# The hybrid mixer in one written order: convolution taps spread over the attention, split scores

## The chip, the cores and the metric

The kernel runs on one core of a Trainium2 chip. The metric is the device time of one execution in microseconds (us), from the first instruction to the last. Its engines each take their own instructions strictly in their own order: PE (TensorE, matrix products; its weight loads are listed as PEld), DVE (VectorE), ACT (ScalarE), POOL (GpSimd) and SP (which here only issues transfers). They wait for each other by semaphores. An instruction that waits holds back everything that stands behind it on its engine.

## The reference

The program is a two layer decoder trunk over 512 tokens of width 1024, all in float32. The change touches one part only, the mixer of layer 0, which is attention beside a convolution module:

```python
def hybrid_mixer(h, cos, sin, w_in, dw_w, dw_b, ln_g, ln_b, w_out):
    proj = h @ w_in
    q = apply_partial_rotary(heads(proj[..., :A_WIDTH]), cos, sin)
    k = apply_partial_rotary(heads(proj[..., A_WIDTH:2 * A_WIDTH]), cos, sin)
    v = heads(proj[..., 2 * A_WIDTH:3 * A_WIDTH])
    for window, dilation in DILATED_PATTERNS:
        o_g, lse_g = dilated_window_branch(q, k, v, window, dilation)
...
    u = proj[..., 3 * A_WIDTH:]
    glu = u[..., :CONV_CHANNELS] * jax.nn.sigmoid(u[..., CONV_CHANNELS:])
    c = causal_depthwise_conv(glu, dw_w) + dw_b
    c = jax.nn.silu(layer_norm(c, ln_g, ln_b))
    return jnp.concatenate([attn, c], axis=-1) @ w_out
```

There are 8 heads of 64 channels, so one tile of 128 partitions holds two heads; the convolution has 31 taps over 512 channels (four tiles). Around this mixer stand four SwiGLU blocks and a gated DeltaNet mixer.

## The kernel before

Activations lie transposed: 128 channels on the partitions and all 512 tokens along the free side, so a row of width 1024 is eight tiles. Every weight matrix product is made in three passes of a faster 32 bit format (fp32r): weights and activations are each split into a high part (a rounding copy on ACT) and a low part (the rest), and `mm3` (lines 138 to 142) adds high by high, high by low and low by high into one PSUM tile. A product of a 128 channel output tile with all 1024 input channels is so 24 matmuls of 512 columns; it is called a projection here. `load_split` (line 120) brings the 128x1024 weights of one projection: a transfer issued on SP into `raw`, the copy `whi` on ACT, its negative into `wlo` on ACT, and a transfer issued on POOL that adds the weights to `wlo` in memory. There are three buffers for `whi` and `wlo`.

The mixer (`hybrid`, `hybrid_heads`) does, in the order of the code: angles for the rotation; eight projections for the convolution, whose gated result goes to `pad`; the 31 taps for tile 0 (`conv31`, lines 740 to 753, each tap one multiply and add on DVE over 128x512); the projection of v with tokens on the partitions (lines 759 to 774); then four turns, one for each tile of two heads. A turn (lines 813 to 860) projects and rotates q and k (`rotary`: a multiplication by the norm `R` on DVE, a swap of channels by a matmul with the matrix `perm`, one multiplication on DVE, a multiplication and a sum on POOL). For each of two heads and four blocks of 128 queries it makes scores (one float32 matmul), adds the mask and takes the negative maximum (one DVE instruction, line 829), the exponential with its sum (ACT, 832), the reciprocal (DVE, 834) and a scaling copy (ACT, 835). Then the probabilities are transposed on PE (843), copied out (ACT, 846), and multiplied with v (852). After turns 0 and 1 the remaining taps follow, after turn 2 the layer norm of the convolution. `out_proj` (line 292) makes eight output projections, adds them to `h`, and prepares the next block's input (`feed`).

PSUM has four tags of two buffers each: `mm` and `po` (projections and outputs), `sc` (scores) and `tr` (rotations and transposes). In the mixer before, nothing fixes the order of the queues beyond what depends on what: the scheduler that lays out the program takes from each engine's ready instructions, so that pieces of projections stand between scores and taps stand between everything. In the blocks around it, `manual_schedule` holds the three engines to the order of the code.

Of the kernel before, what the change touches and what calls it, by code (L numbers as in the profile page):

```python
# [50 lines left out]
def trunk(ctx, tc, io, out, phases):  # L51
# [68 lines left out]
    def load_split(src, n):  # L120
        raw = load(src, n)
        hi = wp.tile([P, 1024], F32R, tag="whi", name=nm("whi"), bufs=NWB)
        lo = wp.tile([P, 1024], F32R, tag="wlo", name=nm("wlo"), bufs=NWB)
        for c in range(0, n, T):
            s = slice(c, min(c + T, n))
            A.activation(hi[:, s], raw[:, s], AF.Copy)  # L126
            A.activation(lo[:, s], hi[:, s].bitcast(F32), AF.Copy, scale=-1.0)
            G.dma_start(lo[:, s], src[:, s], accum_op=ALU.add)
        return [(hi[:, c:c + T], lo[:, c:c + T]) for c in range(0, n, T)]
# [563 lines left out]
    def hybrid(xn, nxt, ahead):  # L693
        with tc.tile_pool(name="ho", bufs=1, side="right", reuse_waits="tile") as op:
            o_x = hybrid_heads(xn, op)
            xn.close()
            out_proj(io["whybo"], o_x, nxt, (0, 1, 2, 4, 5, 6, 7, 3), ahead)

    def hybrid_heads(xn, op):
        with tc.tile_pool(name="hy", bufs=1, side="right", reuse_waits="tile") as hp:  # L700
            def ht(tag, bufs, dt=F32, n=T):
                return hp.tile([P, n], dt, tag=tag, name=nm(tag), bufs=bufs)

            K.update(consts_in(hp, "hcst", HCONSTS))
            pi = hp.tile([P, T], I32, tag="s", name="pi", bufs=7)
            SP.dma_start(pi, io["pos"].to_broadcast([P, T]))
            ang, n_, Ct, St = ht("s", 7), ht("s", 7), ht("Ct", 1), ht("St", 1)
# [9 lines left out]
            V.tensor_mul(Ct, Ct, Ct)  # L717
            V.tensor_scalar(Ct, Ct, -2.0, 1.0, op0=ALU.mult, op1=ALU.add)

            dwh = pr["dww"]  # L720
            V.tensor_scalar(dwh, dwh, 0.5, None, op0=ALU.mult)

            pads = []
            for t in range(4):
                pad = ht("pad", 4, n=30 + T)
                G.memset(pad[:, :30], 0.0)
                pb = proj(io["whyb"][16 + t], xn)
                if t == 0:
                    xn.finish()
                b = tmp("b")  # L730
                V.tensor_mul(b, pb, xn.R)
                A.activation(b, b, AF.Tanh, scale=0.5)
                pa_ = proj(io["whyb"][12 + t], xn)
                a = tmp("a")
                V.tensor_mul(a, pa_, xn.R)
                V.scalar_tensor_tensor(pad[:, 30:], b, 1.0, a, op0=ALU.add, op1=ALU.mult)
                pads.append(pad)

            cv = []

            def conv31(t):
# [7 lines left out]
                V.tensor_scalar(acc, x, w, pr["dwb"][:, t:t + 1], op0=ALU.mult, op1=ALU.add)  # L749
                for j in range(30):  # L750
                    x, w = tap(j)
                    V.scalar_tensor_tensor(acc, x, w, acc, op0=ALU.mult, op1=ALU.add)  # L752
                cv.append(acc)

            for t in (0,):
                conv31(t)

            vps = [psum("po" if i % 2 else "mm") for i in range(NT)]
            for q4 in range(4):
                wt = load_split(io["wv"][q4], 1024)  # L760
                for k2 in range(2):
                    k = q4 * 2 + k2
                    xh, xl = xn.x[k]
                    w_h, w_l = wt[k2]
                    for i in range(NT):
                        s = slice(i * P, (i + 1) * P)
                        PE.matmul(vps[i], xh[:, s], w_h, start=(k == 0), stop=False)
                        PE.matmul(vps[i], xh[:, s], w_l, start=False, stop=False)
                        PE.matmul(vps[i], xl[:, s], w_h, start=False, stop=(k == NK - 1))
            vt = []  # L770
            for i in range(NT):
                v = ht("vt", 4)
                A.activation(v, vps[i], AF.Copy, scale=xn.rcol[:, i:i + 1])
                vt.append(v)

            o_x = [None] * NK

            def rotary(idx, tag):
                ps = proj(io["whyb"][idx], xn)
                q = ht("qk", 2)  # L780
                V.tensor_mul(q, ps, xn.R)
                sw = psum("tr")
                PE.matmul(sw, K["perm"], q, start=True, stop=True)
                t1 = ht("s", 7)
                V.tensor_mul(t1, sw, St)
                qr = ht(tag, 2)
                G.tensor_mul(qr, q, Ct)
                G.tensor_add(qr, qr, t1)
                return qr

            def layer_norm():
                mu = psum("sc")
                tot = ht("s", 7)
                G.tensor_add(tot, cv[0], cv[1])
                G.tensor_add(tot, tot, cv[2])
                G.tensor_add(tot, tot, cv[3])
                PE.matmul(mu, K["o512"].to_broadcast([P, P]), tot, start=True, stop=True)
                acc = ht("s", 7)
                for t in range(4):
                    V.tensor_sub(cv[t], cv[t], mu)  # L800
                    if t == 0:
                        A.activation(acc, cv[t], AF.Square)
                    else:
                        sq = ht("s", 7)
                        A.activation(sq, cv[t], AF.Square)
                        G.tensor_add(acc, acc, sq)
                Rl, _ = token_rstd(acc, K["o512"])
                for t in range(4):
                    V.tensor_mul(cv[t], cv[t], Rl)
                    A.activation(cv[t], cv[t], AF.Silu, scale=pr["lng"][:, t:t + 1],  # L810
                                 bias=pr["lnb"][:, t:t + 1])
                    o_x[4 + t] = split(cv[t], op, "ox", 16)

            for t in range(4):
                qr = rotary(t, "qr")
                kr = rotary(4 + t, "kr")
                po = psum("po")
                for b in range(2):
                    rows = slice(64 * b, 64 * b + 64)
                    pt = [None] * 3  # L820
                    probs = []
                    for i in range(NT):
                        w = (i + 1) * P
                        ps = psum("sc")
                        PE.matmul(ps[:, :w], qr[rows, i * P:(i + 1) * P], kr[rows, :w],  # L825
                                  start=True, stop=True)
                        s = ht("s", 7)
# [483 lines left out]
```

## Time and profile before

| what | us |
|---|---|
| median of 3 runs (lowest, highest) | 2124.0 (2117.0, 2132.3) |
| the profiled execution | 2122.85 |
| span in it, first to last instruction | 2121.0 |
| mixer of layer 0, from its first matmul to the next block's first | 254.5 (384.38 to 638.90) |

A row of the profile names line, engine, operation, output <- inputs with the tile names of the program, shapes, and how many. "Busy" of PE runs to the modelled end of each matmul, so it says little about how densely they follow; the distance between starts does. PEclk is the share of full clock that the chip granted the PE.

### The profile page before, as it was taken

Reading aid. Unit: us, or ns where it says so; the run is one execution under the profiler, and the core shown is the slowest. Engines: PE = TensorE matmul, PEld = TensorE weight load, DVE = VectorE, ACT = ScalarE, POOL = GpSimd, SP = SyncE. Lnnn points to the kernel's source line nnn. Section 1 sums busy time; section 2 is a strip of 40 time slices with the busy share of each in tenths; the row PEclk is TensorE's granted clock in tenths of the full one; section 3 lists DMA queues with packets and bytes.
Section 4 is the critical chain, followed back from the end, with each engine's and each line's share of the span. In section 5 each row is a group of like instructions: output and inputs, shape, how many; then the busy total and the mean of one; then the engine's idle time right before and its main releaser. Section 6 shows DMA issues by size and latency. Waiting matters only on the chain.

```text
span 2121.0 us, 33055 instructions
## 1 busy us (share of the span) xinstructions
PE 2035.4 (96%) x12662; PEld 1779.5 (84%) x12662; DVE 1610.4 (76%) x2758; ACT 1113.4 (52%) x2023; POOL 188.9 (9%) x240
## 2 busy tenths in 40 slices
PE   7999999999999999999999999989989999999997
PEld 6999997875568999987899998767778878999986
DVE  5888879897357888889788888657684477888876
ACT  5444447545564444465444446676454664444455
POOL 0000000332410000000000000233312210000000
PEclk9999999998899999999999999989988999999998
DMA  3333333882343333322333332679735453333321
GB/s 123 102 108 102 109 101 97 180 171 55 66 85 105 109 101 109 110 76 73 108 109 101 109 105 82 177 212 228 150 106 134 103 120 115 100 108 102 103 87 45
DMA packets 112878, 237.71 MB, mean 112 GB/s; under 512 B 22608, under 2 KB 25424, under 8 KB 112720
## 3 DMA queue, kind: packets, MB, share of 16 engines
q1 hardware_dynamic: 90544, 193.06, 29.8%
q0 software_dynamic: 21648, 42.02, 11.1%
q8 instruction: 99, 1.62, 0.3%
q14 instruction: 59, 0.48, 0.1%
q10 hardware_dynamic: 528, 0.52, 0.1%
HBM read 224.55 MB, written 11.01 MB: 111 GB/s over the span
## 4 chain that ended last, share of the span: by engine, by line
PE 80%; DVE 9%; ACT 4%; DMA 3%; issue 3%; POOL 1%; SPq 0%; DVEq 0%; POOLq 0%; ACTq 0%
PE mm L141 12%; PE mm L140 12%; PE mm L142 12%; PE sc L141 7%; PE sc L140 7%; PE sc L142 7%; PE po L141 2%; PE po L142 2%; PE po L140 2%; PE tr L141 2%; PE tr L140 2%; PE tr L142 2%; PE sc L825 1%; DVE wlo L117 1%; DVE gl L386 1%
## 5 line engine op out<-in xcount | busy, mean ns | idle before, releaser
L117 DVE TENSOR_TENSOR wlo<-raw,whi 128x1024 fp32r<-128x1024 f32 (+1 forms) x400 | 473.2, 1201 | 155.8 <-ACT whi L116 154.8
L140 PE MATMUL mm<-xh,whi 128*128 128x256 f32 (+2 forms) x1800 | 563.2, 313 | 9.1 <-ACT b L456 4.0
L142 PE MATMUL mm<-xh,wlo 128*128 128x256 f32 (+2 forms) x1800 | 560.6, 311 | 1.7 <-DMA wlo<-in_wgdn 1.7
L141 PE MATMUL mm<-xl,whi 128*128 128x256 f32 (+2 forms) x1800 | 560.9, 312 | 0.0
L116 ACT ACTIVATE whi<-raw 128x1024 fp32r<-128x1024 f32 (+1 forms) x400 | 404.8, 1034 | 32.4 <-issue 14.3
L140 PEld LDWEIGHTS mm<-xh,whi 128*128 128x128 f32 (+1 forms) x1800 | 343.7, 191 | 47.9 <-ACT b L456 7.2
L141 PEld LDWEIGHTS mm<-xl,whi 128*128 128x128 f32 (+1 forms) x1800 | 343.4, 191 | 30.0 <-issue 3.0
L142 PEld LDWEIGHTS mm<-xh,wlo 128*128 128x128 f32 (+1 forms) x1800 | 343.2, 191 | 21.7 <-issue 3.3
L140 PE MATMUL sc<-xh,whi 128*128 128x256 f32 x1056 | 298.6, 283 | 7.7 <-DVE b L458 3.8
L141 PE MATMUL sc<-xl,whi 128*128 128x256 f32 x1056 | 298.7, 283 | 3.4 <-DVE xl L251 3.4
L142 PE MATMUL sc<-xh,wlo 128*128 128x256 f32 x1056 | 298.3, 282 | 2.0 <-DVE wlo L117 2.0
L140 PEld LDWEIGHTS sc<-xh,whi 128*128 128x128 f32 x1056 | 199.7, 189 | 10.0 <-DVE b L458 5.6
L386 DVE TENSOR_TENSOR gl<-g,gh 128x512 fp32r<-128x512 f32 (+1 forms) x286 | 178.6, 643 | 34.0 <-ACT gh L385 33.3
L141 PEld LDWEIGHTS sc<-xl,whi 128*128 128x128 f32 x1056 | 200.1, 189 | 4.0 <-DVE xl L251 4.0
L142 PEld LDWEIGHTS sc<-xh,wlo 128*128 128x128 f32 x1056 | 200.2, 190 | 2.9 <-DVE wlo L117 2.9
L385 ACT ACTIVATE gh<-g 128x512 fp32r<-128x512 f32 (+1 forms) x286 | 166.3, 591 | 68.9 <-PE mm L141 34.6
L403 ACT ACTIVATE a<-a 128x512 f32<-128x512 f32 x88 | 55.8, 634 | 251.7 <-DVE a L402 251.7
L126 ACT ACTIVATE whi<-raw 128x512 fp32r<-128x512 f32 x137 | 80.3, 623 | 95.1 <-PE mm L141 70.8
L442 ACT ACTIVATE b<-mm 128x256 f32<-128x256 f32 x84 | 32.2, 383 | 152.7 <-PE mm L142 152.7
L456 ACT ACTIVATE b<-mm 128x256 f32<-128x256 f32 x88 | 33.8, 384 | 140.3 <-PE mm L142 140.3
L752 DVE SCALAR_TENSOR_TENSOR cv<-pad,prm_t,cv 128x512 f32<-128x512 f32 x120 | 91.1, 801 | 0.9
L141 PE MATMUL mm<-gl,whi 128*128 128x512 f32 (+1 forms) x220 | 83.2, 378 | 5.1 <-DVE gl L386 4.9
(400 smaller groups left out, 3579.9 us busy)
## 6 DMA issues: line engine op xcount, KB each, us to landing
raw<-in_wf1i SPq DMA_DIRECT2D x82, 512.0 KB, 3.5
raw<-in_wf2i SPq DMA_DIRECT2D x82, 512.0 KB, 3.5
raw<-in_wgdn SPq DMA_DIRECT2D x32, 512.0 KB, 4.8
wlo<-in_wgdn POOLq DMA_DIRECT2D x64, 256.0 KB, 5.7
raw<-in_wf2i SPq DMA_DIRECT2D x56, 256.0 KB, 2.7
raw<-in_wf1i SPq DMA_DIRECT2D x52, 256.0 KB, 2.6
raw<-in_wf1b SPq DMA_DIRECT2D x20, 512.0 KB, 3.5
raw<-in_wf2b SPq DMA_DIRECT2D x20, 512.0 KB, 3.5
```

What stands on the lines that cost most here:

```text
L116: A.activation(hi[:, s], src[:, s], AF.Copy)
L117: V.tensor_sub(lo[:, s], src[:, s], hi[:, s].bitcast(F32))
L126: A.activation(hi[:, s], raw[:, s], AF.Copy)
L140: PE.matmul(ps, whi, xhi, start=first, stop=False, skip_group_check=skip)
L141: PE.matmul(ps, whi, xlo, start=False, stop=False, skip_group_check=skip)
L142: PE.matmul(ps, wlo, xhi, start=False, stop=last, skip_group_check=skip)
L385: A.activation(hi, g[f][:, s], AF.Copy)
L386: V.tensor_sub(lo, g[f][:, s], hi.bitcast(F32))
L403: A.activation(cg[f], cg[f], AF.Silu)
L442: A.activation(b0[f][:, HT:], pb[f][:, :HT], AF.Copy)
L456: A.activation(b1[f][:, :HT], pb[f][:, :HT], AF.Copy)
L752: V.scalar_tensor_tensor(acc, x, w, acc, op0=ALU.mult, op1=ALU.add)
```

## The change

The mixer is written as one fixed order for PE, ACT and DVE under `manual_schedule`. Five things differ.

1. **Weights.** `load_split` can treat 1024 columns at a time, and the mixer does: one `whi`, one `wlo` and one POOL transfer for a projection where there were two of each. All 28 weight tiles stand in one list (`hybrid_weights`); `take(i)` makes sure that i, i+1 and i+2 are loaded. The first two are loaded inside the tail of the block before.
2. **Taps.** All 124 taps come from one generator and are placed by `taps(n)`: 36 in the last three quarters of the convolution's projections, 28 in the projection of v, 4 ahead of the first turn and 56 in the first three turns.
3. **Turns as a pipeline.** A turn projects q and k of the next turn, rotates this turn's k and the next q, finishes the values of the previous turn, and then makes this turn's scores. The rotation takes the PSUM tile twice (ACT copies it to `qa` for the swap matmul; DVE multiplies it with `Ct`, in which `R` is already contained), and its sum and multiplications are now on DVE. q and k are split into high and low parts.
4. **Scores.** Three fp32r passes with 64 channels instead of one float32 matmul; one reciprocal for four blocks.
5. **Layer norm and output.** The layer norm runs in five pieces placed in the last turn, its sums on DVE instead of POOL. The first two output projections are begun before the last turn's values, for all channels but the last attention tile.

```diff
-    def load_split(src, n):
+    def load_split(src, n, step=T):
...
+        def take(i, n=3):
+            for j in range(i, min(i + n, len(srcs))):
+                if j not in got:
+                    got[j] = load_split(srcs[j], 1024, 1024)
+            return got[i]
...
+            else:
+                taps(6)
...
+            pa_ = project(2 * t + 1, None if t else xn.rows)
...
+            taps(7)
...
+        def raw_rows(i):
+            ps = project(i)
+            qa = ht("qa", 2)
+            A.activation(qa, ps, AF.Copy)
+            u = ht("u", 2)
+            V.tensor_mul(u, ps, Ct)
+            return qa, u
+
+        def rotate(q, tag, bufs):
+            qa, u = q
+            sw = psum("tr")
+            PE.matmul(sw, K["perm"], qa, start=True, stop=True)
+            t1 = ht("t1", 1)
+            V.tensor_mul(t1, sw, St)
+            V.tensor_add(u, u, t1)
+            hi, lo = ht(tag + "h", bufs, F32R), ht(tag + "l", bufs, F32R)
+            A.activation(hi, u, AF.Copy)
+            V.tensor_sub(lo, u, hi.bitcast(F32))
+            return hi, lo
...
+                PE.matmul(ps[:, :w], qh[rows, c], kh[rows, :w], start=True, stop=False)
+                PE.matmul(ps[:, :w], qh[rows, c], kl[rows, :w], start=False, stop=False)
+                PE.matmul(ps[:, :w], ql[rows, c], kh[rows, :w], start=False, stop=True)
...
+        q = raw_rows(12)
+        k = raw_rows(13)
+        taps(4)
+        qr = rotate(q, "q", 2)
...
+        for t in range(NT):
+            if t < 3:
+                q = raw_rows(14 + 2 * t)
+                taps(6)
+            else:
+                next(ln)
+            kr = rotate(k, "k", 1)
+            if held:
+                values(t - 1, 0, *held)
+            if t < 3:
+                k = raw_rows(15 + 2 * t)
+                taps(6)
+                qn = rotate(q, "q", 2)
+            else:
+                next(ln)
+            if held:
+                values(t - 1, 1, *held)
+                o_x[t - 1] = split(held[1], op, "ox", 16)
+            taps(5)
+            if t == 3:
+                next(ln)
+            probs = scores(t, qr, kr)
+            if t == 3:
+                next(ln)
+            qr = qn
+            held = probs, psum("po")
+        taps(99)
+        next(ln, None)
+        for b in range(2):
+            out_ps[b] = psum("mm")
+            out_mm(out_ps[b], take(20 + b, 2), o_x, (0, 1, 2, 4, 5, 6, 7), True, False)
+            values(3, b, *held)
+        o_x[3] = split(held[1], op, "ox", 16)
```

Three places show what became of the order, all in the turns. Names: `mm`, `tr`, `sc`, `po` are PSUM tiles; `cv` is a tap's sum; `qk`, `u` are q or k before the rotation is complete, `s`, `t1` the swapped part times the sine; `pt` are copied transposes; the number at the end of a name tells tiles apart.

DVE in the second turn before, from the multiplication of the projected q (L781) to the first mask (L829):

```order
L781 TENSOR_TENSOR qk_796_4895<-mm_792_4860,R_658_4120 128x512
L752 SCALAR_TENSOR_TENSOR cv_863_5079<-pad_687_4319,prm_t_67,cv_863_5079 128x512 x2
L834 RECIPROCAL rd_776_4756<-den_775_4754 128x1
L752 SCALAR_TENSOR_TENSOR cv_863_5079<-pad_687_4319,prm_t_67,cv_863_5079 128x512
L834 RECIPROCAL rd_781_4766<-den_780_4764 128x1
L752 SCALAR_TENSOR_TENSOR cv_863_5079<-pad_687_4319,prm_t_67,cv_863_5079 128x512 x5
L785 TENSOR_TENSOR s_798_4899<-tr_797_4897,St_647_4045 128x512
L135 TENSOR_TENSOR lo_789_4793<-po_735_4665,hi_788_4792 128x512
```

DVE in the second turn after the change, from the projected q (L853) to the first mask (L885):

```order
L853 TENSOR_TENSOR u_798_4901<-mm_796_4874,Ct_653_4060 128x512
L778 SCALAR_TENSOR_TENSOR cv_723_4583<-pad_684_4260,prm_t_67,cv_723_4583 128x512 x6
L861 TENSOR_TENSOR t1_800_4911<-tr_799_4909,St_654_4061 128x512
L862 TENSOR_TENSOR u_759_4764<-u_759_4764,t1_800_4911 128x512
L865 TENSOR_TENSOR kl_802_4915<-u_759_4764,kh_801_4914 128x512
L853 TENSOR_TENSOR u_814_4975<-mm_812_4948,Ct_653_4060 128x512
L774 TENSOR_SCALAR cv_815_4977<-pad_695_4344,prm_t_67 128x512
L778 SCALAR_TENSOR_TENSOR cv_815_4977<-pad_695_4344,prm_t_67,cv_815_4977 128x512 x5
L861 TENSOR_TENSOR t1_817_4986<-tr_816_4984,St_654_4061 128x512
```

In both, taps stand between the use of the projection and the reading of the swap's PSUM tile (`tr`); after the change six of them stand behind each of the two projections, and the sum of the rotation, which was on POOL, follows on DVE.

PE in the second turn before, where its scores (L825) begin while the next projection (`mm_864`) runs:

```order
L140 MATMUL mm_864_5111<-xh_584_3802,whi_866_5114 128x512
L825 MATMUL sc_809_4949<-kr_807_4945,qr_799_4901 128x128
L825 MATMUL sc_814_4959<-kr_807_4945,qr_799_4901 128x256
L141 MATMUL mm_864_5111<-xl_585_3803,whi_866_5114 128x512
L142 MATMUL mm_864_5111<-xh_584_3802,wlo_867_5115 128x512
L825 MATMUL sc_819_4969<-kr_807_4945,qr_799_4901 128x384
L825 MATMUL sc_824_4979<-kr_807_4945,qr_799_4901 128x512
L843 MATMUL tr_829_4989<-cst_69,s_810_4951 128x128
```

PE in the second turn after the change, from the end of the projection of q (`mm_796`) to the next projection (`mm_812`):

```order
L142 MATMUL mm_796_4874<-xh_647_4037,wlo_746_4682 128x512
L859 MATMUL tr_799_4909<-qa_758_4762,hcst_4054 128x512
...
L913 MATMUL tr_803_4918<-cst_69,s3_778_4818 128x128
L913 MATMUL tr_805_4925<-cst_69,s1_772_4802 128x128
...
L913 MATMUL tr_807_4932<-cst_69,s3_778_4818 128x128
L921 MATMUL po_792_4866<-pt_804_4923,vt_724_4586 64x512
...
L921 MATMUL po_792_4866<-pt_806_4930,vt_727_4592 64x128
L140 MATMUL mm_812_4948<-xh_512_3534,whi_755_4732 128x512
```

Projections now stand whole, and between two of them stand the swap, three `tr` tiles of transposes and the products with v. Since `tr` has two buffers, the tiles take them in turn: `tr_799`, `tr_803`, then `tr_805` in the buffer of `tr_799`, then `tr_807` in that of `tr_803`.

ACT in the same stretch after the change (there is no such row before, where the rotation's last step was on POOL):

```order
L851 ACTIVATE qa_797_4899<-mm_796_4874 128x512
L864 ACTIVATE kh_801_4914<-u_759_4764 128x512
L916 ACTIVATE pt_804_4923<-tr_803_4918 128x512
L916 ACTIVATE pt_806_4930<-tr_805_4925 128x512
L916 ACTIVATE pt_808_4935<-tr_807_4932 128x256
L126 ACTIVATE whi_810_4943<-raw_809_4941 128x1024
```

The copy of the rotated k (`kh_801`) now stands ahead of the copies of the transposes, and the program makes the multiplication `u_798` on DVE wait for the copy `qa_797` of the same PSUM tile.

More of the change, by code (lines that the diff above doesn't have):

```diff
@@ L752, in conv31 @@
                     V.scalar_tensor_tensor(acc, x, w, acc, op0=ALU.mult, op1=ALU.add)
+                    yield
                 cv.append(acc)
[L755 to L769, printed above, removed]
@@ L791, in layer_norm @@
[L791 to L812, printed above, removed]
@@ L859, in hybrid_heads, with taps, project @@
-            return o_x
+        conv = conv31()
+        def taps(n):
+            for _ in range(n):
+                next(conv, None)
+        def project(i, mid=None):
+            wt = take(i)
+            ps = psum("mm")
+            for k in range(NK):
+                hi, lo = wt[k // 4]
+                c = slice(k % 4 * P, k % 4 * P + P)
+                mm3(ps, hi[:, c], lo[:, c], xn.x[k], k == 0, k == NK - 1)
+                if mid and k == 3:
+                    mid()
+            return ps
```

284 lines of the change are left out of this document (187 added, 97 removed).

## The prediction

> **What bounds the kernel now.** First the page's busy times and the shares of its chain of work, then the mixer cut into stages: convolution with v up to the first turn, four turns, output.
>
> ```profile
> PE 2035.4 (96%) x12662; PEld 1779.5 (84%) x12662; DVE 1610.4 (76%) x2758; ACT 1113.4 (52%) x2023; POOL 188.9 (9%) x240
> ...
> PE 80%; DVE 9%; ACT 4%; DMA 3%; issue 3%; POOL 1%; SPq 0%; DVEq 0%; POOLq 0%; ACTq 0%
> ```
>
> ```profile
> core 0: us, PE busy (x) PEld busy (x) DVE busy (x) ACT busy (x) POOL busy (x), PEclk, DMA share, GB/s
> 384.40:459.30 74.90, 74.64 (x330) 60.41 (x329) 71.36 (x119) 36.39 (x66) 22.80 (x26) 1.00 0.88 183
> 459.30:509.60 50.30, 45.81 (x146) 26.21 (x144) 38.29 (x65) 22.02 (x48) 19.17 (x16) 0.83 0.40 85
> 509.60:538.20 28.60, 27.21 (x104) 15.56 (x104) 17.72 (x42) 16.22 (x39) 9.00 (x8) 1.00 0.35 73
> 538.20:580.40 42.20, 38.42 (x126) 21.52 (x126) 16.62 (x48) 26.04 (x53) 16.18 (x14) 0.81 0.30 58
> 580.40:604.00 23.60, 23.60 (x88) 12.71 (x89) 7.58 (x29) 12.37 (x32) 0.00 (x0) 0.98 0.00 0
> 604.00:638.90 34.90, 33.57 (x142) 26.17 (x141) 26.95 (x46) 21.77 (x36) 8.71 (x10) 1.00 0.64 131
> ```
>
> The mixer is 254.5 us, the sum of the rows, and PE sets it: busy to the end in every stage, since the scheduler fills each wait with pieces of a projection. What an in-order program does depends on what an empty PE waits for. One wait stands out before, the scores after the rotation's sum on POOL, 4.6 us in three places:
>
> ```profile
> PE sc L825 <- POOL kr L788: 4.6, 3, 1.8
> ```
>
> And two turns run at a lower clock. Inside the first of them, columns as above:
>
> ```profile
> 470.00:475.00 5.00, 3.19 (x14) 1.86 (x12) 5.00 (x10) 0.31 (x2) 3.23 (x4) 1.00 0.64 109
> ...
> 480.00:485.00 5.00, 5.00 (x11) 2.27 (x10) 1.49 (x5) 2.13 (x6) 0.00 (x0) 0.50 0.00 0
> ...
> 490.00:495.00 5.00, 5.00 (x18) 2.53 (x17) 3.77 (x6) 3.60 (x9) 1.06 (x1) 0.73 0.01 3
> ```
>
> After a stretch with 1.81 us of PE idle (5.00 less 3.19) the clock stands at half although PE never rests.
>
> **Unit prices.** From the timeline (start, duration; distances between starts are taken):
>
> ```profile
> 384.38 0.40 PE L140 MATMUL mm<-xh,whi 128*128 128x512 f32 x1
> ```
>
> ```profile
> 627.70 0.39 PE L140 MATMUL mm<-hi,whi 128*128 128x512 f32 x1
> ...
> 638.90 0.28 PE L140 MATMUL mm<-xh,whi 128*128 128x256 f32 x1
> ```
>
> The first is the mixer's first matmul. Between the other two lie the last 48 matmuls, 11.20 us: 0.233 each, 5.60 for a projection of 24.
>
> ```profile
> 499.14 1.13 PE L783 MATMUL tr<-qk,hcst 128*128 128x512 f32 x2
> 500.19 0.86 PE L852 MATMUL po<-pt,vt 128*64 128x256 f32 x4
> ...
> 516.73 1.12 PE L825 MATMUL sc<-kr,qr 64*128 64x512 f32 x2
> 517.78 0.55 PE L843 MATMUL tr<-cst,s 128*128 128x128 f32 x3
> ...
> 521.71 0.77 PE L843 MATMUL tr<-cst,s 128*128 128x128 f32 x5
> 522.23 0.48 PE L140 MATMUL mm<-xh,whi 128*128 128x512 f32 x1
> ...
> 594.27 2.37 PE L852 MATMUL po<-pt,vt 128*64 128x512 f32 x8
> 596.57 0.55 PE L843 MATMUL tr<-cst,s 128*128 128x128 f32 x3
> ```
>
> The swap matmul takes 1.05, a widest float32 score 1.05, five transposes 0.52, the four products of one head with v 2.30 (each float32 matmul is two records).
>
> ```profile
> 435.22 23.94 DVE L752 SCALAR_TENSOR_TENSOR cv<-pad,prm_t,cv 128x512 f32<-128x512 f32 x36
> ```
>
> ```profile
> 397.05 0.69 DVE L731 TENSOR_TENSOR b<-mm,R 128x512 f32<-128x512 f32 x1 [0.47 <-ACT R L288]
> 397.65 0.68 DVE L735 TENSOR_TENSOR a<-mm,R 128x512 f32<-128x512 f32 x1
> ```
>
> ```profile
> 557.31 1.09 ACT L846 ACTIVATE pt<-tr 128x512 f32<-128x512 f32 x2 [1.80 <-PE tr L843]
> ```
>
> A tap is 0.665 (23.94 / 36), six are 3.99; any other DVE row of 512 is 0.60 and an ACT copy 0.55. The masks, two of each width in a turn, and what ACT does with weights and with the silu, by groups:
>
> ```profile
> L829 DVE CUSTOM_DVE_ANT_0 s<-sc,hcst 128x512 f32<-128x512 f32 x8 | 5.5, 690 | 6.9 <-PE sc L825 6.9
> L829 DVE CUSTOM_DVE_ANT_0 s<-sc,hcst 128x384 f32<-128x384 f32 x8 | 4.5, 558 | 5.1 <-PE sc L825 5.1
> L829 DVE CUSTOM_DVE_ANT_0 s<-sc,hcst 128x256 f32<-128x256 f32 x8 | 3.4, 422 | 6.3 <-PE sc L825 6.0
> L829 DVE CUSTOM_DVE_ANT_0 s<-sc,hcst 128x128 f32<-128x128 f32 x8 | 2.3, 284 | 8.1 <-PE sc L825 8.1
> ...
> L116 ACT ACTIVATE whi<-raw 128x1024 fp32r<-128x1024 f32 x8 | 8.3, 1047 | 0.0
> L126 ACT ACTIVATE whi<-raw 128x512 fp32r<-128x512 f32 x51 | 29.8, 623 | 49.9 <-PE mm L141 36.9 <-PE po L769 10.4 <-DMA raw<-in_whybo 1.5
> ...
> L810 ACT ACTIVATE cv<-cv,prm_t 128x512 f32<-128x512 f32 x4 | 3.2, 807 | 1.1 <-DVE cv L809 1.1
> L810 ACT ACT_TABLE_LOAD x1 | 1.3, 1283 | 0.0
> ...
> L128 POOL DMA_DIRECT2D wlo<-in_whyb x28 | 24.6, 955 | 49.5 <-ACT wlo L127 38.5 <-ACT pt L846 10.4 <-issue 0.4
> L788 POOL TENSOR_TENSOR kr<-kr,s 128x512 f32<-128x512 f32 x4 | 6.5, 1634 | 2.5 <-DVE s L785 2.5
> ```
>
> **The change, part by part.**
>
> *Weights, whole tiles.* Two copies of 623 ns become one of about 1047 on ACT, and POOL loses an issue of 955 ns per projection. Neither engine sets the end of the first stage (36.39 and 22.80 busy of 74.90), so 0. The early loads also give 0: the mixer's first matmul follows its forerunner without a gap. SP keeps its number of loads.
>
> *Front.* Eight projections and v's four are 12 x 5.60 = 67.2 us. The stage of before, 74.90, ends a little into the next projections. The DMA share of 0.88 there leaves little slack, and DVE is no bound (36 taps, 24 us, lie under 33 us of projections). Between 67.2 and 74.9 I take 71.
>
> *First turn.* PE runs four projections and three swaps: 22.4 + 3.15 = 25.6. The scores then fill the two `sc` buffers and wait for the first mask, and before that mask stand on DVE, in order: the use of the last projection (its copy `qa` 0.55, on ACT behind weight copies for some 1.3, and u 0.60), six taps 3.99, t1 and the sum 1.2, the high copy 0.55 and the low part 0.60, five taps 3.33. That is 12.1, less the 1.05 of the swap: 11.1. The masks pace the scores, 2 x (0.690 + 0.558 + 0.422 + 0.284) = 3.9, 4.3 with hand-offs. Together 41.
>
> *Second and third turn, each half.* From the end of a projection: qa 0.55, u 0.60, taps 3.99, t1 0.60, with hand-offs 6.2 us until the `tr` buffer of the swap is read. PE has put the swap and four transposes (1.05 + 0.42) into the two `tr` buffers and now stands, with the next projection behind it. Then 0.42 for the second tile of transposes; ACT, which has held the copies of the transposes behind that of the rotated k, does the sum's copy and `pt` (sum 0.60, 2 x 0.55), 2.0 in all up to the first product; products with the last copy 2.5. With the projection 5.6 + 6.2 + 2.0 + 2.5 = 16.3. PE works 5.60 + 1.05 + 10 transposes 1.04 + 2.30 = 10 of them.
>
> A turn has two halves (32.6), 1.3 for `qa` behind weight copies, the split of the finished values and five taps ahead of the first mask (0.55 + 0.60 + 3.33 = 4.5, 4.7 with hand-offs), scores 4.3: 42.9, twice 85.8.
>
> *Scores in three passes.* Three times 0.233 is 0.70 against 1.05 at 512 columns: 0.35 at most for each wide one. The masks pace them, so 0 on the path; without masks, 8 x 0.35 = 2.8 less. The sum moved from POOL (6.5 us) is counted above at 0.60 each.
>
> *Last turn and output.* The layer norm's second statistic stands ahead of values(2,1) on PE. Before it: three sums 1.8, the first statistic 1.05, k's rotation 2.95, four differences and three sums 4.2, four squares 2.2, values(2,0) 3.3 and ACT's end of the exponentials, partly side by side: 12 to 18, I take 17. Then the second values and the split 5, scores 5, silu with its table 1.283 + 4 x 0.807 and splits 4 x 1.15 (9.1, of which the scores and the `Rl` multiplications cover about 2) 7, two output blocks of 21 matmuls 9.8, two heads' values in series with ACT's copies 2 x 6, last split and six matmuls 2.6, six projections 33.6, and the fourth weight, whose buffers come free late, about 4. Sum 96, with 88 (statistic at 12, weight hidden) to 104 (as far upward).
>
> *Sum.* 71 + 41 + 85.8 + 96 = 293.8 against 254.5: +39.3.
>
> *Clock.* The price of half clock for these waits is in no row directly. A projection at half clock costs up to 5.60 more; there are eight dense stretches behind waits of 4 us or more (the rows show a fall behind 1.81). From below 0 (and before already lost some: 0.17 of 50.3 and 0.19 of 42.2, at most 16.6 us of full-speed work, which could come back), from above 30. I take 1.4 each, 11, nearer the low end because half the mixer's long waits lie beside a DVE path that PE's pace does not set.
>
> The Trainium skill ("TensorE: Matmul & The Clock Gate", Part 1) has a rule that speaks against the change: an idle window of about 3.4 us halves PE's clock and a busy one of the same length restores it. By it each of eight waits would cost one window at half speed, an estimate of 8 x 1.7 = 14 us from that page, and the sum would be 2176. This trace agrees with the half (0.50) but not with the return: at 480 to 485 PE has been busy for over 5 us and the clock is still 0.50.
>
> The profiled execution took 2122.85 us, 1.15 below the median 2124.0 of the runs. 2122.85 + 39.3 + 11 = 2173.
>
> **Rivals.**
> 1. *Faster: the order keeps PE full.* Decides if the taps fit under PE's own work between swap and second transposes, 1.47 us; then a half-turn is 10 us. PE alone: 71 + four projections, swaps (44.8 + 8 x 1.05), values 8 x 3.34, scores about 16, output 44.8 and 3 for the last split: 215, 39 less, 2083. For it: scores need no POOL. Against: six taps need 3.99. Chance 0.08.
> 2. *The waits are there, the clock stays full*: 2122.85 + 39.3 = 2162. For it: the turn at 509.60 ran at 1.00 in spite of a wait. Chance 0.25.
> 3. *Half clock everywhere behind waits and a late weight*: 39.3 + 30 + 10 = 2202. For it the 0.50 rows; against it, the 1.00 of the front. Chance 0.15.
> 4. *Nearly no change*: the waits are half as long, since taps pair with PE's gaps, since taps run while PE still works: half of 39.3, 2142. For it: taps ran at 0.665 beside POOL, and may be nearer the 0.60 of other DVE rows; against it, only 0.4 us of a wait of 4.7 go so. Chance 0.10.
>
> **How the numbers follow.** The main case has 0.42; its own range is 2155 to 2192. About 1% (21 us) is what a measurement of this kernel tells from no change. Rivals 2 and 3 and the main case are all slower, 0.82; rival 1 faster, 0.08; of rival 4 all is counted as same, 0.10. The range 2130 to 2208 leaves out rival 1, the lower half of rival 4 and the far end of rival 3: 0.08 + 0.05 + 0.05.
>
> **What would show it.** In the profile after: idle of PE ahead of the transposes put down to DVE `t1` or ACT `pt`, about 5 us, four times; idle ahead of the scores of about 10 us in the first turn; DVE's masks directly behind taps; PE's share of the chain below 80% and DVE's above 9%; PEclk below 1.00 in more than two stages; the mixer near 300 us and everything outside it unchanged. Wrong would be: PE idle under 1 us ahead of the transposes, taps shorter than 0.5 us, or a mixer below 255 us.

## The result and the profile after

The changed kernel took 2200.8 us (median of 4 runs, 2198.7 to 2202.6) against 2120.5 beside it: a ratio of 1.0368 with a 95% interval of 1.0323 to 1.0413, so it is slower. 2173 was forecast, with a range of 2130 to 2208. The profiled execution took 2202.54 us, 79.7 more than that of before. The mixer, from its first matmul at 386.58 to the next block's first at 720.49, grew from 254.5 to 333.9 us, 79.4 more: all of the loss lies in it.

The busy times and the shares of the chain of work of the changed kernel:

```profile
PE 2046.9 (93%) x12694; PEld 1807.2 (82%) x12694; DVE 1620.7 (74%) x2758; ACT 1116.9 (51%) x1981; POOL 133.7 (6%) x190
...
PE 75%; DVE 10%; issue 8%; ACT 4%; DMA 2%; POOL 0%; SPq 0%; DVEq 0%; ACTq 0%; POOLq 0%
```

DVE and ACT work nearly as much as before (10.3 and 3.5 us more), and PE is 11.5 us busier. Most of the 80 us is not work. The stages show what they are. The rows are: the front to the end of v, the first turn to its last score, the second, the third, the last turn to its last score, then two pieces of the output:

```profile
core 0: us, PE busy (x) PEld busy (x) DVE busy (x) ACT busy (x) POOL busy (x), PEclk, DMA share, GB/s
386.60:461.20 74.60, 69.39 (x306) 56.82 (x305) 65.12 (x103) 31.98 (x37) 10.37 (x12) 0.98 0.75 173
461.20:509.50 48.30, 31.67 (x127) 24.62 (x125) 28.80 (x52) 18.68 (x33) 3.45 (x4) 0.80 0.42 94
509.50:561.50 52.00, 34.93 (x113) 23.01 (x112) 23.66 (x46) 18.33 (x40) 1.73 (x2) 0.70 0.18 41
561.50:614.00 52.50, 35.98 (x113) 23.47 (x112) 23.86 (x46) 18.27 (x40) 1.73 (x2) 0.70 0.17 40
614.00:652.00 38.00, 23.86 (x74) 14.56 (x74) 15.63 (x45) 15.42 (x38) 0.00 (x0) 0.63 0.00 0
652.00:686.50 34.50, 29.44 (x116) 20.01 (x117) 11.22 (x21) 20.76 (x33) 1.73 (x2) 0.92 0.17 46
686.50:720.50 34.00, 30.10 (x122) 23.52 (x121) 21.05 (x34) 16.32 (x21) 3.46 (x4) 0.95 0.55 110
```

In the turns no engine is busy for three quarters of the time: each waits for another. From the view of waits, what PE waited for between the end of v and the next block (us in all, times, longest):

```profile
PE sc L880 <- DVE m L885: 26.2, 8, 13.0
PE tr L913 <- DVE t L861: 21.1, 4, 5.3
PE tr L913 <- ACT pt L916: 5.9, 9, 1.0
PE sc L929 <- DVE t L928: 4.3, 1, 4.3
PE tr L942 <- DVE t L939: 4.2, 1, 4.2
PE po L142 <- DMA wlo<-in_whybo: 3.9, 1, 3.9
PE mm L140 <- ACT hi L134: 3.8, 2, 3.1
PE sc L880 <- ACT kh L864: 2.7, 1, 2.7
```

One of the four waits of 5.3 us, from the timeline of the second turn (start, duration; idle time before in brackets, with what ended it):

```profile
518.25 0.69 DVE L853 TENSOR_TENSOR u<-mm,Ct 128x512 f32<-128x512 f32 x1 [6.28 <-ACT qa L851]
518.28 0.60 PE L913 MATMUL tr<-cst,s 128*128 128x128 f32 x4
518.86 4.68 DVE L778 SCALAR_TENSOR_TENSOR cv<-pad,prm_t,cv 128x512 f32<-128x512 f32 x6
523.45 0.68 DVE L861 TENSOR_TENSOR t<-tr,St 128x512 f32<-128x512 f32 x1
524.17 0.69 DVE L862 TENSOR_TENSOR u<-u,t 128x512 f32<-128x512 f32 x1
524.19 1.11 PE L913 MATMUL tr<-cst,s 128*128 128x128 f32 x4 [5.32 <-DVE t L861]
```

PE has made the swap and one tile of transposes, and the next tile needs the buffer of the swap. DVE reads it only behind six taps, from 518.86 to 523.45. Whatever stands behind it on PE, the products with v and the next projection, waits too. The four waits are 5.32, 5.18, 5.31 and 5.32 us long.

### The profile page after: what moved, and what is told of

It reads as the page before. It is cut to its first block, busy times and chain, and to the rows that moved or that the text cites. A ratio compares the mean times of both kernels' runs of the same rounds, so it can differ in the third digit from the quotient of the medians.

```text
span 2200.7 us, 32961 instructions
## 1 busy us (share of the span) xinstructions
PE 2046.9 (93%) x12694; PEld 1807.2 (82%) x12694; DVE 1620.7 (74%) x2758; ACT 1116.9 (51%) x1981; POOL 133.7 (6%) x190
## 4 chain that ended last, share of the span: by engine, by line
PE 75%; DVE 10%; issue 8%; ACT 4%; DMA 2%; POOL 0%; SPq 0%; DVEq 0%; ACTq 0%; POOLq 0%
PE mm L141 12%; PE mm L140 12%; PE mm L142 12%; PE sc L141 7%; PE sc L140 7%; PE sc L142 7%; PE po L142 2%; PE po L140 2%; PE po L141 2%; PE tr L140 2%; PE tr L142 2%; PE tr L141 2%; DVE cv L778 1%; DVE wlo L117 1%; DVE gl L386 1%
## 5 line engine op out<-in xcount | busy, mean ns | idle before, releaser
L140 PE MATMUL sc<-xh,whi 128*128 128x256 f32 x1056 | 301.0, 285 | 12.6 <-ACT whi L116 5.5
L126 ACT ACTIVATE whi<-raw 128x512 fp32r<-128x512 f32 (+2 forms) x109 | 76.7, 732 | 59.1 <-PE mm L141 36.9
```

The lines of the kernel that those rows point to most:

```text
L140: PE.matmul(ps, whi, xhi, start=first, stop=False, skip_group_check=skip)
```

## The experiments

Twelve kernels were run in four groups; the kernel before was run beside each group (medians 2120.6, 2126.9, 2122.8 and 2134.7), so across groups the ratios are compared. Lengths of the mixer are from one profiled execution of each kernel: 254.5 before, 333.9 after. The runs of the kernel before spread over some 30 us (2107.6 to 2138.6 in the second group), so differences of a few us between such lengths are weak.

**1. Six taps behind the rotation instead of inside it.**

```diff
                 q = raw_rows(14 + 2 * t)
-                taps(6)
...
             kr = rotate(k, "k", 1)
+            if t < 3:
+                taps(6)
...
-                taps(6)
                 qn = rotate(q, "q", 2)
+                taps(6)
```

> The two groups of six taps in each of the first three turns stand behind the rotation instead of ahead of its reading of the swap's PSUM tile. Theory (the taps hold that tile, and so PE): the waits of PE for t1 fall from 21.1 us to about 5, the first scores' wait for the rotated k (2.7) goes, and some of the half clock with them: 16 to 28 us less than the changed kernel, 2172 to 2186. Rival (the wait only moves: the late taps stand ahead of the masks): the wait of the scores for the masks grows from 26 us to about 42, time stays at 2195 to 2205.

Measured: 2172.3 us, ratio 1.0257 (1.0226 to 1.0289), mixer 307.2. Its waits:

```profile
PE sc L880 <- DVE m L885: 27.9, 8, 14.6
...
PE tr L913 <- DVE t L861: 3.1, 5, 0.7
```

The wait for t1 went (21.1 to 3.1), and the wait for the masks did not take it over (26.2 to 27.9): the late taps run while PE multiplies the values. So 18 us of wait, and a mixer 26.7 us shorter: the place of 36 taps in three turns, worth about a third of the loss.

**2. As the first, and the five taps ahead of the masks put behind the scores.**

```diff
-            taps(5)
...
             probs = scores(t, qr, kr)
+            taps(5)
```

> As the kernel with late taps, and the five taps ahead of the masks stand behind the scores. Theory: the wait for the masks falls from 26 to about 8 us as well (three times 3.8 and what the late groups added), the clock of the turns rises above 0.8: 30 to 55 us less than the changed kernel, 2146 to 2171. Rival (PE is held by the rest of the chain, rotation and copies, and the taps fill time that is lost anyway): no more than 12 us less, above 2188.

Measured: 2165.4 us, ratio 1.0221 (1.0194 to 1.0248), mixer 296.4.

```profile
PE sc L880 <- DVE m L885: 16.2, 7, 10.7
...
PE sc L929 <- DVE t L928: 7.4, 1, 7.4
```

The time is as expected, the wait for the masks is not: 16.2 instead of about 8, of which 10.7 in the first turn, where the rotation of the next q still stands on DVE ahead of the first mask. The layer norm's first sum came later instead (4.3 to 7.4), since the last taps now reach into the last turn: the mixer gained 10.8 us against the kernel with late taps, the whole kernel 6.9 by the medians. What is left, 42 us more than before, is in many small places.

**3. The same instructions without the fixed order.** The `manual_schedule` of the mixer is left out, nothing else.

> The changed mixer's instructions without the fixed order of the three engines: the scheduler lays them out as it did before. Theory (the order makes the loss, not the instructions): the time returns to 2105 to 2140, PE's waits for t1 and for the masks fall below 10 us together. Rival (the instructions cost it: three passes per score, sums on DVE, rows that wait for copies): above 2170.

Measured: 2099.8 us, ratio 0.9921 (0.9889 to 0.9952), mixer 239.5, which is 15 us less than before and 94 less than in the written order. Its longest waits of PE in the turns:

```profile
PE sc L879 <- ACT kh L863: 0.7, 1, 0.7
PE sc L879 <- DVE m L884: 0.5, 2, 0.3
```

The time is 5 us below the expected 2105 to 2140. This settles the main question: instructions, buffers and places in the code are the same, so the written order alone costs 94 us of mixer, and what it orders is by itself a little faster than the kernel before. Not all of the slow clock went with the order, though. It is full between 480 and 540 us and at half again from 550 on, in the last turn, behind waits of 0.73 us at most:

```profile
480.00:500.00 20.00, 20.00 (x87) 13.93 (x88) 18.55 (x40) 15.36 (x35) 1.73 (x2) 1.00 0.42 89
550.00:555.00 5.00, 5.00 (x17) 3.03 (x17) 2.03 (x12) 2.63 (x8) 0.00 (x0) 0.50 0.00 0
```

**4. Idle matmuls in the waits.** To price the clock apart from the waits, PE got matmuls whose result nobody reads.

```diff
+        def fill(tag, n):
+            ps = psum(tag)
+            for _ in range(n):
+                PE.matmul(ps, xn.x[0][0][:, :P], xn.x[1][0], start=True, stop=True)
...
             for js in ((0,), (1, 3), (2,)):
+                if js == (1, 3) and t < 2:
+                    fill("sc", 16)
...
             for i in range(NT):
+                if i == 2:
+                    fill("tr", (36, 14, 11, 8)[t])
                 score(0, i)
```

> The changed kernel with idle matmuls added, whose result nobody reads: 16 of 512 columns in each of the four waits for t1 of the second and third turn, 36, 14, 11 and 8 in the waits for the first mask of the four turns. Nothing else is moved, and no wait is taken away. Theory (half clock behind the waits costs about 9 us a turn beyond the waits): PEclk of the second and third turn rises from 0.70 to above 0.9 and the time falls by 12 to 28 us, 2173 to 2189. Rival (the clock is not on the path, the waits alone make the time): no change or slower, 2197 to 2212.

Measured: 2192.3 us, ratio 1.0346 (1.0319 to 1.0374), mixer 321.1. The second and third turn, cut at this kernel's own last scores:

```profile
core 0: us, PE busy (x) PEld busy (x) DVE busy (x) ACT busy (x) POOL busy (x), PEclk, DMA share, GB/s
508.20:553.90 45.70, 38.72 (x159) 27.33 (x158) 23.67 (x46) 17.48 (x38) 1.73 (x2) 0.95 0.21 46
553.90:601.10 47.20, 39.18 (x156) 28.23 (x155) 23.96 (x46) 19.01 (x42) 1.73 (x2) 0.90 0.20 45
```

The clock rose as expected (0.70 to 0.95 and 0.90), the gain was below the expected 12 to 28 us: 8.5 by the medians, 12.8 in the profiles. A turn lost 6.3 and 5.3 us, not 9. By the ratios the intervals of this kernel and of the changed one overlap (1.0319 to 1.0374 against 1.0323 to 1.0413), so the gain rests on the profiles. What is left of a turn's length is, as far as is shown, waits that a faster PE does not shorten. In these profiles half clock costs time, and it is the smaller part.

**5. More of them, in the first and the last turn.** As the fourth, with 9 and 46 in the first turn and 14, 14 and 10 in the last, in the waits for the rotated k and the first mask, ahead of the two statistics and ahead of the first output projection.

> As the changed kernel with idle matmuls, and more of them: 9 in the first turn's wait for the rotated k, 46 there in the wait for the first mask, and 14, 14 and 10 in the last turn ahead of the two layer norm statistics and the first output projection. No wait is taken away. Theory (half clock costs in every turn what it cost in the second and third): another 5 to 9 us less than with the first idle matmuls, 2183 to 2188. Rival (in the last turn the chain is on DVE and ACT, so that PE's clock is worth nothing there): 2189 to 2196.

Measured: 2188.2 us, ratio 1.0298 (1.0256 to 1.0339), mixer 317.3. It falls between the two expectations and the intervals of both filled kernels overlap; this one also touches that of the changed kernel (1.0339 against 1.0323). In the profiles another 3.8 us came back. All fillers together: 333.9 to 317.3, 16.6 us of clock that could be had back this way by the profiles, 12.6 by the medians. The clock was not full everywhere even so: it stood at 0.76 between 600 and 640 us.

**6. DVE free, PE and ACT in the written order.** The set of engines of `manual_schedule` is cut.

```diff
-                tc.manual_schedule(engines={nc.tensor.engine, nc.scalar.engine, nc.vector.engine}):
+                tc.manual_schedule(engines={nc.tensor.engine, nc.scalar.engine}):
```

> The changed kernel with the written order kept for PE and ACT only, and DVE laid out by the scheduler. Theory (DVE's written order, with taps ahead of what PE waits for, is what holds PE): the waits for t1 fall from 21.1 to about 6 us, those for the masks from 26.2 to about 8, those for the layer norm's sums by half, and the clock rises: 40 to 60 us less than the changed kernel, 2140 to 2162. Rival (PE's own written order, without a projection to fill a wait, is what costs): 2170 or more, since the rotation still stands between the projections.

Measured: 2133.3 us, ratio 1.0048 (1.0015 to 1.0081), mixer 269.3. On DVE the taps now stand around the rotation:

```profile
509.83 0.68 DVE L853 TENSOR_TENSOR u<-mm,Ct 128x512 f32<-128x512 f32 x1
510.43 0.68 DVE L861 TENSOR_TENSOR t<-tr,St 128x512 f32<-128x512 f32 x1
511.03 0.74 DVE L778 SCALAR_TENSOR_TENSOR cv<-pad,prm_t,cv 128x512 f32<-128x512 f32 x1
511.69 0.69 DVE L862 TENSOR_TENSOR u<-u,t 128x512 f32<-128x512 f32 x1
```

From the use of the projection to t1 it is 0.60 us; in the written order above it was 5.20 (518.25 to 523.45). The waits of PE for the masks and t1:

```profile
PE sc L880 <- DVE m L885: 3.7, 7, 0.7
PE tr L913 <- DVE t L861: 2.7, 5, 0.8
```

The time is 7 us below the expected 2140 to 2162. With PE and ACT as strict as in the change, 64.6 of the 94 us are gone.

**7. PE free, DVE and ACT in the written order.** The set without `nc.tensor.engine`.

> The changed kernel with the written order kept for ACT and DVE only, and PE laid out by the scheduler. Theory (a PE that may take the next projection's matmuls during a wait loses nothing to the taps): waits for t1 below 5 us, 2110 to 2150. Rival (DVE's order sets the pace by itself, whatever PE does): the waits for the masks and t1 stay above 30 us together and the time above 2165.

Measured: 2179.9 us, ratio 1.0279 (1.0225 to 1.0334), mixer 311.2. The rival held in its time, above 2165: with DVE's order kept, a free PE finds other work for some of its waits, and then stands elsewhere.

```profile
PE mm L140 <- DVE u L853: 12.5, 2, 6.3
PE sc L880 <- DVE m L885: 8.7, 5, 4.5
PE mm L142 <- DMA wlo<-in_whyb: 7.7, 3, 3.3
```

The first row is a projection that waits for its PSUM tile, which DVE reads late. The rival's other sign, more than 30 us of waits for masks and t1, did not come: the masks are at 8.7 and t1 is not among the long waits. Runs 6 and 7 together: freeing DVE is worth 65 us of mixer, freeing PE 23. ACT's order alone was not freed.

**8. Taps of two tiles in turn.** The generator of the taps steps tiles 0 and 1, then 2 and 3, alternately (after the first 12).

```diff
+            for t in (0, 2):
+                a = chain(t)
...
+                live = [a, chain(t + 1)]
+                while live:
+                    for c in list(live):
...
+                            next(c)
```

> The changed kernel with the taps in another order: after the first 12, the taps of two channel tiles take turns, so that no tap adds to the sum that the tap ahead of it wrote. Same taps, same places. Theory (a tap that takes the sum of the one ahead starts 0.787 us after it, one that doesn't 0.665): the waits for t1 fall from 21.1 to about 18 us, those for the masks from 26.2 to about 23.5, 4 to 7 us in all: 2192 to 2198. Rival (the distance has another cause, such as PE or DMA traffic in the turns): distance stays 0.787, 2198 to 2203.

Measured: 2195.9 us, ratio 1.0356 (1.0299 to 1.0412), whose interval does not part it from the changed kernel; mixer 327.4, 6.5 us shorter. Six taps in a turn:

```profile
516.72 4.06 DVE L779 SCALAR_TENSOR_TENSOR cv<-pad,prm_t,cv 128x512 f32<-128x512 f32 x6
```

They take 4.06 instead of 4.68 us, while one tap lasts about as long, so the distance fell from 0.787 to 0.665 ((4.68 - 0.75) / 5 and (4.06 - 0.74) / 5). The waits for t1 and the masks fell to 19.0 and 24.8. The cause of the distance is shown; that it saves total time is likely, not shown.

**9. Without order, and one float32 matmul per score.** q and k are not split.

```diff
-                PE.matmul(ps[:, :w], qh[rows, c], kh[rows, :w], start=True, stop=False)
-                PE.matmul(ps[:, :w], qh[rows, c], kl[rows, :w], start=False, stop=False)
-                PE.matmul(ps[:, :w], ql[rows, c], kh[rows, :w], start=False, stop=True)
+                PE.matmul(ps[:, :w], qh[rows, c], kh[rows, :w], start=True, stop=True)
```

> The mixer without the fixed order (as in the kernel without order), and the scores as one float32 matmul again, so that q and k are not split. Theory (with PE full, the passes are worth what they save on PE, 0.35 us for 512 columns, 1.75 us a turn): 4 to 9 us slower than the kernel without order, 2103 to 2110. Rival (the masks pace the scores, and the splits on ACT and DVE cost as much): within 3 us of it, 2096 to 2103.

Measured: 2103.8 us, ratio 0.9896 (0.9864 to 0.9927) in its group against 0.9921 (0.9889 to 0.9952) for three passes in theirs; mixer 232.3. In microseconds this lies at the near edge of the expected loss (2103 to 2110), but the groups differ; the ratios overlap and lean the other way. These runs show no loss from one pass, so the split passes gain nothing that was measured, even with PE full.

**10. As the ninth, the first output projections begun early,** for two attention tiles ahead of the last turn, and the taps in turn.

> The mixer without the fixed order, scores in one float32 matmul, taps of two tiles in turn, and the first two output projections begun for the first two attention tiles ahead of the last turn, where no projection is left to fill PE's waits. Theory (what is left of the loss in the last turn is empty PE and its half clock, and 12 matmuls of 0.233 us, twice 1.4 us, fill it): 2 to 8 us less than the kernel without order and with one pass, a ratio to the kernel before of 0.983 to 0.989. Rival (the scheduler already takes these matmuls early): no change, 0.988 to 0.992.

Measured: 2103.7 us, ratio 0.9888 (0.9852 to 0.9924), mixer 234.2. The ratio lies where both expectations overlap (0.988 to 0.989), so it does not decide between them; against the ninth (0.9896) no change is shown.

**11. The kernel before, with one instruction moved.** The rotation's sum runs on DVE.

```diff
-                G.tensor_add(qr, qr, t1)
+                V.tensor_add(qr, qr, t1)
```

> The kernel before with one instruction moved: the rotation's last sum runs on DVE and not on POOL. Theory (this is the part of the change that gains: PE's three waits of 4.6 us for it, and the half clock that follows them): 4 to 14 us less than before, ratio 0.993 to 0.998. Rival (the gain of the instructions lies elsewhere, as DVE is then late with taps or masks): ratio 0.998 to 1.003.

Measured: 2096.7 us, ratio 0.9863 (0.9817 to 0.991), mixer 234.0, 20.5 less than before, more than the theory allowed. In the kernel before, POOL issued two transfers ahead of the sum:

```profile
470.18 1.76 POOL L128 DMA_DIRECT2D wlo<-in_whyb  x2
470.70 0.68 DVE L785 TENSOR_TENSOR s<-tr,St 128x512 f32<-128x512 f32 x1
471.53 1.70 POOL L788 TENSOR_TENSOR kr<-kr,s 128x512 f32<-128x512 f32 x1
```

That queue hardly mattered: the sum's other input `s` was finished at 471.38, and the sum began 0.15 us later. Its own length did, 1.70 us on POOL, where with the sum on DVE it is 0.68 and PE's wait for it shrinks to one of 0.5 us:

```profile
472.63 0.68 DVE L788 TENSOR_TENSOR kr<-kr,s 128x512 f32<-128x512 f32 x1
```

```profile
PE sc L825 <- DVE kr L788: 0.5, 1, 0.5
```

The wait for POOL was 4.6 us in three places, and the two slow stages of before lost at most 16.6 us to the clock (0.17 of 50.3 and 0.19 of 42.2): 21.2 together, near the 20.5 gained. That the waits brought the slow clock is likely, not shown. The first two turns before, and with the sum on DVE:

```profile
461.00:488.00 27.00, 24.18 (x68) 13.10 (x66) 20.32 (x40) 9.80 (x23) 8.93 (x8) 0.77 0.37 81
488.00:518.00 30.00, 28.30 (x102) 16.20 (x103) 23.25 (x48) 16.29 (x39) 9.46 (x8) 0.92 0.34 71
```

```profile
461.00:488.00 27.00, 26.28 (x106) 16.45 (x104) 25.50 (x54) 17.27 (x40) 9.01 (x8) 1.00 0.54 105
488.00:518.00 30.00, 29.87 (x115) 16.55 (x114) 24.72 (x52) 18.38 (x44) 6.83 (x7) 1.00 0.34 76
```

The clock (third number from the end) is 1.00 where it was 0.77 and 0.92, although the wait ahead of the scores had been under 2 us each time.

**12. The change without order, and the sum back on POOL.**

```diff
-            V.tensor_add(u, u, t1)
+            G.tensor_add(u, u, t1)
```

> The changed mixer without the fixed order, and the rotation's sum back on POOL, where it was before. Theory (of the changed instructions this sum alone gains): PE waits for POOL ahead of the scores again, about 1.5 us a time, with half clock behind it, and the time returns to that of the kernel before, ratio 0.996 to 1.003. Rival (the other edits, weights in whole tiles, the three passes, the layer norm in pieces, gain by themselves, or the wait is gone since the product is on DVE): ratio 0.986 to 0.994.

Measured: 2114.1 us, ratio 0.9924 (0.9888 to 0.996), mixer 237.0: as without order and with the sum on DVE. The rival held. The sum is not the only way to this gain: here the product is already on DVE and POOL issues half as many weight transfers, and PE's longest wait ahead of the scores was 1.2 us for the copy of k, which itself waited for POOL's sum. The kernels 3, 11 and 12 have one thing in common, a clock of 1.00 between 480 and 540 us, where the kernel before stood at half for a time. Which of the remaining edits is enough for it was not parted.

## Why the prediction came out as it did

**The mechanism was right.** PE waits for t1 four times, 5.2 to 5.3 us each where 4.7 was worked out; the masks stand behind taps, with 13.0 us ahead of the first where about 10 was named; the first statistic's wait and the copies of transposes are there. Without the dependence on six taps the wait went (run 1), and without the order the waits for t1 and the masks were all but gone (run 3). PE's share of the chain fell below 80% and DVE's rose above 9%, as named. The layer norm's second statistic began 17.9 us into the last turn (631.89 less 614.0), for 17 taken.

**The size was too small: 50.3 us of mixer forecast (39.3 and 11 of clock), 79.4 measured, so 29 missing.** The mixer was to come out near 300 us and took 333.9. At 2200.8 the time lies outside the main case's own range (2155 to 2192); it is inside 2130 to 2208 only because the whole range was drawn wide enough for the rival with half clock, and that is luck. By stages: front 74.6 for 71, first turn 48.3 for 41, two turns 104.5 for 85.8, last turn and output 106.5 (720.5 less 614.0) for 96; that is 40.1, of which 11 had been set aside for the clock. Where it was mis-sized:

- *The clock,* 11: the fillers returned 16.6 us, 5.6 more, and they did not reach every place (0.90 to 0.95 is left in the middle turns of run 4, 0.76 between 600 and 640 us in run 5). In the two middle turns the fillers alone returned 11.6.
- *The price of a tap,* 0.665: that row had come from a stretch in which taps of two tiles, by their distance, took turns. The change runs one tile's taps in a row, at 0.787; so did the kernel before while only its first tile was begun (five taps in 3.90 us at 399.91). Run 8 returned 6.5 us of mixer for it.
- *The front,* 71: 3.6 short, near its upper bound of 74.9; PE waits 4.05 us there for one weight transfer, 1.16 for the gate.
- *The first turn:* the scores waited 2.7 us for the rotated k and 0.4 for its low part ahead of the wait for the masks, which the sum did not have. 3.1 us. The timeline shows the overlap that was missed: k's rotation was itself still behind six taps (481.75 to 486.35), and on ACT its copy stood ahead of the copy `qa` of the last projection. That copy began at 490.36, 5.6 us after the projection's last matmul, where 1.3 was taken for its delay.
- The rest, 29.1 - 5.6 - 6.5 - 3.6 - 3.1 = 10.3, lies mostly in the last turn, where values and scores were priced at full clock. They took 9.6 us, with the second statistic in it, and 10.2 us, for 5 and 5 (PEclk 0.54 and 0.63). In the scores 2.8 us are a wait for the first mask, which stood on DVE behind eleven small steps of the layer norm (642.85 to 644.89); the sum did not have it. How much of the rest is clock and how much the copies on ACT was not parted.

These parts are from single profiles and partly overlap; they show the order of the terms, not tenths.

**The rivals.** The faster one fell with the waits themselves, and so did the one with nearly no change. The faster one's sum names four projections beside its 44.8 us; that price is of the eight which the four turns have. The one with a full clock would have given 2162. The run with most fillers was 2188 with the clock still short of full, so by how much the waits alone exceed the sum was not measured; that they exceed it is seen in t1 (5.3 for 4.7). The rival with half clock everywhere named 2202, next to the 2200.8 measured, but by the wrong parts: of its 30 us of clock the fillers gave back about 17, and the late weight was 3.9 for its 10. That the number agreed is no support for it.

**The steps costed at nothing.** Three passes: run 9 agrees, though without the order. The moved sum was given 0.60 on a path and no gain elsewhere; run 11 shows that in the kernel before moving it is worth 20.5 us of mixer. Whether that gain is also in the change is not shown: without the order, the sum on DVE and on POOL give the same ratio (0.9921 and 0.9924). The 4.6 us wait of before was read as small; the half clock in the same two stages, which nearly all went with it in run 11, cost up to 16.6 us more and was not counted with it.

**The version that beats both** is the kernel before with that one instruction on DVE: 0.9863 of the kernel before (0.9817 to 0.991). The changed mixer without its order (0.9921) and with one pass (0.9896) overlap with it, so among them nothing is decided, but one moved instruction is the smaller change.

## What to carry to other kernels

If an order is written by hand, look at each buffer that two engines share and list what stands on the reading engine between the producer and the read: filler work such as these taps belongs behind the read that frees a buffer, not ahead of it. Free one engine's order at a time to learn whose order costs: here mostly DVE's (65 us of mixer, PE's 23), although PE does the waiting. Before a large rewrite, move the single instruction that the longest wait names, and count the slow clock behind a wait with the wait.

## What the hardware showed that was not expected

- In these taps, a multiply-add of DVE that takes the sum of the instruction just ahead of it starts 0.787 us after it; with another sum between, 0.665. The durations of the two cases read alike (0.75 and 0.74), so only starts show it.
- A wait of under 2 us of PE was followed in the kernel before by half clock for about 17 us of work without gaps (0.50 between 478 and 488), and a wait of 1.70 us at 509.63 was not. With a wait of 0.5 (run 11) the clock stayed at 1.00, and in run 3 it fell to half behind waits of at most 0.73. What decides between them stays open. In the changed kernel, behind the wait that ended at 524.19, the clock came back within about 8 us of dense work (products from 526.68 on):

```profile
524.00:529.00 5.00, 4.05 (x9) 1.75 (x10) 1.52 (x3) 3.78 (x6) 0.00 (x0) 0.50 0.01 2
529.00:534.00 5.00, 5.00 (x18) 3.33 (x17) 0.00 (x0) 0.21 (x1) 0.86 (x1) 0.75 0.90 205
534.00:537.00 3.00, 3.00 (x15) 2.49 (x14) 0.00 (x0) 0.00 (x0) 0.00 (x0) 1.00 0.05 8
```

  The Trainium skill ("TensorE: Matmul & The Clock Gate", Part 1) has the clock return after a busy window of about 3.4 us. A mean of 0.75 from 529 to 534 puts the return near 531.5, some 5 us after the products began, so the rule holds here within about 2 us. It does not hold for the slow stretch of the kernel before if all of PE's work there, scores and transposes among it, counts as busy; that was not tried.
- Idle matmuls in a wait brought the PE clock from 0.70 to 0.95, and a turn from 52.0 us to 45.7. With more of them (run 5) the kernel took at most 2191.2 us, where the changed kernel, in another group, took at least 2198.7.
